# Sums of weight blocks moved beside their own unit's low parts, a cast in two pieces, parts of the first normed columns out of the engines' sequence

## The chip, the cores and the metric

One core of one Trainium2 chip runs the whole program. The metric is the device time of one execution in microseconds, as the median of several runs. One further execution was profiled; the rows below come from it. PE is TensorE (PEld its weight loads), DVE is VectorE, ACT is ScalarE, POOL is GpSimd, SP is SyncE, whose queue issues nearly all transfers.

## What is computed

The reference is one layer of an encoder block on 256 rows of 2048 columns in float32: a half-step feed-forward part, a mixer (causal pooling and gated linear attention), cross attention to 256 memory rows, a second half-step feed-forward part, and a last norm.

```python
x = x + 0.5 * swiglu(rms_norm(x, ffn1_norm[l]), ffn1_w_gate[l], ffn1_w_up[l], ffn1_w_down[l])
h = rms_norm(x, mix_norm[l])
proj = h @ w_in[l]
...
x = x + jnp.concatenate([y_pool, y_gla], axis=-1) @ w_out[l]
x = x + mem_cross_attention(rms_norm(x, xattn_norm[l]), rms_norm(mem, mem_norm[l]),
                            xattn_w_q[l], xattn_w_kv[l], xattn_w_o[l])
x = x + 0.5 * swiglu(rms_norm(x, ffn2_norm[l]), ffn2_w_gate[l], ffn2_w_up[l], ffn2_w_down[l])
...
def swiglu(h, w_gate, w_up, w_down):
    return (jax.nn.silu(h @ w_gate) * (h @ w_up)) @ w_down
```

The feed-forward width is 5632. All weights are float32; 417.58 MB are read from memory in all.

## The kernel before

**Units.** The weights come in as units of 1 MB: a raw tile of 128 partitions by 2048 float32 columns, fetched by SP's queue (L570) into one of three raw buffers. A matmul works on two parts of a number: a high part in the format fp32r and a low part, the remainder. Of a *plain* unit, ACT casts the high part `wh` (L253), DVE subtracts it from the raw weights to make the low part `wl` (L254), and PE does 24 matmuls of 512 columns (L336): high by high, high by low, low by high. `wh` and `wl` have three buffers each, and the split runs two units ahead of the matmuls (`AHEAD`).

**Seven-product units.** In a block of eight units (1024 output columns over 2048 rows of weights), the units of the pairs 0, 2, 4 and 6 are computed by seven block products in place of eight, as in Strassen's scheme: 21 matmuls (L462) in place of 24. For this the weights' four 512-column blocks have to be summed. DVE makes the sums `T` in three additions (L431, one of 1024 and two of 512 columns). The unit's raw blocks 1 to 3 are split as `xh` (ACT) and `xl` (DVE), and `T` as `wh` (ACT) and `wl` (DVE); these last two use the same buffers as a plain unit's. The products P1, P2 and P3 need `xh` and `xl`; P4 to P7 need the parts of `T`. There are 98 such units. The block's order is 0, 1, 2, 3, 4, 6, 5, 7, so seven-product and plain units mostly alternate. At the block's end `combine` (L518 to L523) puts the partial products together and `join` (L533) adds or subtracts them from what the plain units gathered.

**What sets the order.** `Stream` holds the units and the operations between them, in the order of the program. `emit` goes through them and calls, two units ahead of the matmuls, `prepare`, which makes the sums `T` of the *following* unit, and then `split` of the unit itself. So, where a plain unit is followed by a seven-product one, `T` of the latter comes first on DVE, then `wl` of the plain unit; only between two seven-product units is it the other way round. After the split the load of the unit three later is issued; its raw buffer comes free once the split's last reader is done. `in_turn` ties each of these instructions on ACT and DVE behind the one before it. `behind_weights` ties another operation behind the last of them on both engines, and `among_weights` makes it a link of that sequence, so that the splits that come later also stand behind it. What isn't tied is placed by a scheduler.

**Where norms are folded in.** `fold` (L718 to L735) transposes 512 columns of x into a PSUM bank `px` (8 small matmuls, L724) and scales them into high and low parts `xs` (four pairs of L222 on ACT and L223 on DVE). It is called for four chunks of columns, c = 0 to 3, two of them (eight pairs) after the residual of each 1024-column block, and runs beside the next block's units. Its parts are `among_weights`. `Sums.make` builds the sums of activations that the seven products need (`x_sums.make`, called for each of four pairs after a number of units). `gain_columns` clears a tile on DVE (L615) and has a queue fetch gains into it. A first block of the first feed-forward part calls `amid` at one of its quarters.

Of the kernel before, what the change touches and what calls it, by code (L numbers as in the profile page):

```python
# [8 lines left out]
F32R = mybir.dt.float32r  # L9
# [5 lines left out]
P = 128  # L15
# [18 lines left out]
class Stream:  # L34
# [23 lines left out]

    def unit(self, load, f, split=None, prepare=None):
        self.items.append((len(self.units), f))  # L60
        self.units.append((load, split, prepare))
        self.pending = [(n - 1, h) for n, h in self.pending]
        self._flush()

    def emit(self, load, prepare, split):
        done, w, late = -1, {}, []
        for u, f in self.items:
            if u is None:
                f()
                continue  # L70
            ahead = min(u, 1) if u < self.FIRST else self.AHEAD
            while done < min(u + ahead, len(self.units) - 1):
                done += 1
                while late:
                    late.pop(0)()
                after = self.units[done + 1][2] if done + 1 < len(self.units) else None
                both = after and self.units[done][2]
                if not both:
                    prepare(done + 1, after)
                w[done], rest = split(done, self.units[done][1])  # L80
                if both:
                    prepare(done + 1, after)

                def finish(done=done, rest=rest):
                    if rest:
                        rest()
                    if done + self.RAW < len(self.units):
                        load(done + self.RAW)

                if rest:  # L90
                    late.append(finish)
                else:
                    finish()
            f(*w.pop(u))


def build(ctx, tc, I, out):
# [240 lines left out]
    def block_t(srcs, act, evict, delays=(0, 0), amid=None):  # L338
# [6 lines left out]
        def unit(gi):  # L345
            def fn(wh, wl):
                if gi == 0:
                    held["ps"] = [ptile(uid("pt")) for _ in range(2)]
                wh, wl = (w.rearrange("p (k j n) -> p k j n", j=2, n=NB) for w in (wh, wl))
                quarters = [(j, kk) for j in range(2) for kk in range(2)]  # L350
                if amid is not None and gi == 0:
                    quarters.sort(key=lambda q: q[1])
                for n, (j, kk) in enumerate(quarters):
                    if amid is not None and n == (1 if gi else 2):
                        amid(gi)
                    k = 2 * gi + kk
                    for h in range(2):
                        products(held["ps"][j][:, h, :], act, k, h, wh[:, kk, j], wl[:, kk, j],
                                 k == 0, k == n_k - 1)
# [18 lines left out]
    class Sums:  # L378
# [6 lines left out]
        def make(self, g):  # L385
# [18 lines left out]
            )  # L404
            nc.vector.tensor_tensor(out=p12, in0=p12, in1=p22, op=ALU.add)
            done = split(self.tile[:, i, 0], self.tile[:, i, 1], a[:, 4 - n :])
            if self.over:
                done = split(act[:, 2 * g, 0, P:], act[:, 2 * g, 1, P:], p11)
            return done

# [10 lines left out]

    def add_weights(u, raw):
        t = seven_tile("T", 4 * NB, F32, u, 1)
        w = raw.rearrange("p (b n) -> p b n", n=NB)
        v = t.rearrange("p (b n) -> p b n", n=NB)
        for o, a, b in (
            (v[:, 0:2], w[:, 1:3], w[:, 0:1].to_broadcast([P, 2, NB])),
# [3 lines left out]
            in_turn("vector", lambda: nc.vector.tensor_tensor(out=o, in0=a, in1=b, op=ALU.add))  # L431
        return t

    def split_seven(u, raw, t):
        th, tl = (
            wpool.tile([P, 4 * NB], F32R, tag=n, name=f"{n}{u}", bufs=st.AHEAD + 1)
            for n in ("wh", "wl")
        )
        r = [seven_tile(n, 3 * NB, F32R, u, 2) for n in ("xh", "xl")]
        split_weights(*r, raw[:, NB:])  # L440
        split_weights(th, tl, t)
        parts = [x.rearrange("p (b n) -> p b n", n=NB) for x in (th, tl, *r)]

        return [parts], None

# [20 lines left out]
    def block_s(srcs, act, sums, order, evict, merge=None, sevens=None):  # L466
# [71 lines left out]
        for g in order:  # L538
            if g in sevens:
                st.unit(srcs[g], unit_s(g), split_seven, add_weights)  # L540
                if g == sevens[-1]:
# [70 lines left out]
    def gain_columns(names, queue):  # L612
        t = rows["gain"] = scope["pool"].tile([P, P], F32, tag="gain", name=uid("gain"), bufs=2)
        if len(names) > 1:
            behind_weights(lambda: nc.vector.memset(t, 0.0))  # L615
        for name, at, n in names:
# [101 lines left out]
    def fold(c, gain):  # L718
# [12 lines left out]

        among_weights(parts)
        for h in range(2):
# [36 lines left out]
    def ffn(wg, wu, wd, down, amid=None):  # L770
# [37 lines left out]
        for i, g in enumerate(PAIRS):  # L808
            st.op(lambda g=g: among_weights(lambda: x_sums.make(g)), (5, 7, 9, 10)[i])
        for lo, n in FF_PARTS:  # L810
# [610 lines left out]

    raws, summed = {}, {}

    def prepare(u, f):
        if f:
            summed[u] = f(u, raws[u])

# [4 lines left out]
    def split_unit(u, own):  # L1432
        raw = raws.pop(u)
        if own is split_seven:
            return split_seven(u, raw, summed.pop(u))
        parts = [
# [18 lines left out]
    for u in range(st.RAW):  # L1455
        load(u)
    st.emit(load, prepare, split_unit)

# [31 lines left out]
```

## Time and profile before

| what | value |
| --- | --- |
| median of 3 runs | 2138.07 us (2137.77 to 2140.59) |
| profiled execution | 2141.02 us |
| its span, first to last instruction | 2138.9 us |
| mean granted TensorE clock | 0.996 of full speed |
| transfers | 435.95 MB, 204 GB/s on the mean |
| DVE waiting for ACT before `wl` of raw weights | 251.1 us |
| ACT waiting for DVE before the cast of `T` | 186.9 us |

The profile gives, for each engine, the time in which it executes. PE's matmuls are pipelined: one of 512 columns is listed with about 0.39 us, while the next starts 0.23 us after it, so PE's pace is read from starts, not from lengths. "Idle before" an instruction is the time its engine did nothing, with the instruction that ended the wait. An engine that isn't the one waited for may be idle at no cost. In the rows, `wl<-raw,wh` means that `wl` is written from `raw` and `wh`; L253 and the like are lines of the kernel.

### The profile page before, as it was taken

Reading aid. Unit: us, or ns where it says so; the run is one execution under the profiler, and the core shown is the slowest. Engines: PE = TensorE matmul, PEld = TensorE weight load, DVE = VectorE, ACT = ScalarE, POOL = GpSimd, SP = SyncE. Lnnn points to the kernel's source line nnn. Section 1 sums busy time; section 2 is a strip of 40 time slices with the busy share of each in tenths; the row PEclk is TensorE's granted clock in tenths of the full one; section 3 lists DMA queues with packets and bytes.
Section 4 is the critical chain, followed back from the end, with each engine's and each line's share of the span. In section 5 each row is a group of like instructions: output and inputs, shape, how many; then the busy total and the mean of one; then the engine's idle time right before and its main releaser. Section 6 shows DMA issues by size and latency. Waiting matters only on the chain.

```text
span 2138.9 us, 24386 instructions
## 1 busy us (share of the span) xinstructions
PE 2099.3 (98%) x9916; PEld 1746.6 (82%) x9916; DVE 1707.2 (80%) x1538; ACT 1092.8 (51%) x986; POOL 14.1 (1%) x40
## 2 busy tenths in 40 slices
PE   9999999999999999999999999999999999999998
PEld 7778887788888888887888888788778887888886
DVE  6999899988997576677666555769998899989974
ACT  7554455544544545364645434546454555445544
POOL 0000000000000000000000000000000000000001
PEclk9999999999999999999999999999999999999999
DMA  7556665566656565457654555565567655776573
GB/s 256 178 182 231 236 216 196 178 235 236 213 200 237 199 197 183 156 193 243 236 190 160 170 165 172 182 233 178 197 216 236 215 198 172 238 239 216 197 256 118
DMA packets 143608, 435.95 MB, mean 204 GB/s; under 512 B 9860, under 2 KB 13544, under 8 KB 143112
## 3 DMA queue, kind: packets, MB, share of 16 engines
q1 hardware_dynamic: 143464, 434.38, 60.0%
q8 instruction: 78, 1.28, 0.2%
q14 instruction: 34, 0.28, 0.0%
q10 hardware_dynamic: 32, 0.01, 0.0%
HBM read 417.58 MB, written 16.78 MB: 203 GB/s over the span
## 4 chain that ended last, share of the span: by engine, by line
PE 69%; DVE 19%; DMA 6%; issue 3%; ACT 3%; SPq 0%; DVEq 0%; ACTq 0%
PE pt L336 32%; PE pa L321 15%; PE pt L462 9%; DVE wl L254 7%; PE pb L336 6%; DVE T L431 5%; PE pe L336 3%; DMA raw<-in_ffn_w_gate 3%; DMA raw<-in_ffn_w_up 2%; DVE xl L254 2%; ACT wh L253 2%; DVE sg L533 1%; DVE sg L520 1%; DVE sg L793 1%; PE pl L1221 1%
## 5 line engine op out<-in xcount | busy, mean ns | idle before, releaser
L254 DVE TENSOR_TENSOR wl<-raw,wh 128x2048 fp32r<-128x2048 f32 (+2 forms) x284 | 637.9, 2250 | 251.7 <-ACT wh L253 251.1
L253 ACT CAST wh<-raw 128x2048 fp32r<-128x2048 f32 (+2 forms) x284 | 532.4, 1881 | 411.1 <-PE pt L336 216.6
L336 PE MATMUL pt<-wh,xs 128*128 128x512 f32 x1536 | 496.7, 392 | 0.0
L336 PE MATMUL pt<-wh,ys 128*128 128x512 f32 x1440 | 451.5, 391 | 0.0
L336 PEld LDWEIGHTS pt<-wh,xs 128*128 128x128 f32 x1536 | 288.8, 188 | 59.5 <-ACT wh L253 0.2
L336 PEld LDWEIGHTS pt<-wh,ys 128*128 128x128 f32 x1440 | 271.4, 189 | 56.2
L321 PE MATMUL pa<-xs,wh 128*128 128x512 f32 x896 | 315.9, 397 | 0.0
L253 ACT CAST wh<-T 128x2048 fp32r<-128x2048 f32 x98 | 187.5, 1913 | 227.3 <-DVE T L431 186.9
L336 PE MATMUL pt<-wl,xs 128*128 128x512 f32 x768 | 300.8, 392 | 1.1 <-DVE wl L254 1.1
L336 PE MATMUL pt<-wl,ys 128*128 128x512 f32 x720 | 282.0, 392 | 0.0
L321 PE MATMUL pa<-xs,wl 128*128 128x256 f32 x896 | 248.5, 281 | 0.0
L254 DVE TENSOR_TENSOR wl<-T,wh 128x2048 fp32r<-128x2048 f32 x98 | 224.0, 2286 | 13.5 <-ACT wh L253 13.2
L321 PEld LDWEIGHTS pa<-xs,wh 128*128 128x128 f32 x896 | 167.6, 188 | 38.1 <-issue 0.3
L253 ACT CAST xh<-raw 128x1536 fp32r<-128x1536 f32 x98 | 145.1, 1480 | 97.9 <-DMA raw<-in_ffn_w_gate 52.7
L254 DVE TENSOR_TENSOR xl<-raw,xh 128x1536 fp32r<-128x1536 f32 x98 | 171.5, 1750 | 5.0 <-ACT xh L253 5.0
L336 PEld LDWEIGHTS pt<-wl,xs 128*128 128x128 f32 x768 | 144.8, 189 | 31.7 <-DVE wl L254 2.0
L321 PEld LDWEIGHTS pa<-xs,wl 128*128 128x128 f32 x896 | 169.1, 189 | 1.7 <-issue 0.2
L336 PEld LDWEIGHTS pt<-wl,ys 128*128 128x128 f32 x720 | 136.1, 189 | 28.3
L431 DVE TENSOR_TENSOR T<-raw 128x1024 f32<-128x1024 f32 x98 | 119.7, 1221 | 33.7 <-DMA raw<-in_ffn_w_gate 17.3
L462 PE MATMUL pt<-wh,xs 128*128 128x512 f32 x320 | 126.4, 395 | 16.2 <-ACT wh L253 14.9
L431 DVE TENSOR_TENSOR T<-T,raw 128x512 f32<-128x512 f32 x196 | 135.2, 690 | 5.3
L462 PE MATMUL pt<-wh,xe 128*128 128x512 f32 x320 | 123.2, 389 | 0.0
(236 smaller groups left out, 2346.4 us busy)
## 6 DMA issues: line engine op xcount, KB each, us to landing
raw<-in_ffn_w_down SPq DMA_DIRECT2D x88, 1024.0 KB, 5.6
raw<-in_ffn_w_up SPq DMA_DIRECT2D x80, 1024.0 KB, 5.1
raw<-in_ffn_w_gate SPq DMA_DIRECT2D x77, 1024.0 KB, 5.1
raw<-in_w_in SPq DMA_DIRECT2D x32, 1024.0 KB, 5.3
raw<-in_xattn_w_kv SPq DMA_DIRECT2D x32, 1024.0 KB, 5.2
raw<-in_w_out SPq DMA_DIRECT2D x16, 1024.0 KB, 5.6
raw<-in_xattn_w_q SPq DMA_DIRECT2D x16, 1024.0 KB, 5.6
raw<-in_xattn_w_o SPq DMA_DIRECT2D x16, 1024.0 KB, 5.7
```

The lines of the kernel that those rows point to most:

```text
L253: in_turn("scalar", lambda: nc.scalar.copy(hi, src))
L254: in_turn("vector", lambda: nc.vector.tensor_tensor(out=lo, in0=src, in1=f32(hi), op=ALU.subtract))
L321: nc.tensor.matmul(o, w, x, start=k == 0 and i == 0, stop=last and i == 1)
L336: nc.tensor.matmul(ps, a, w, start=first and i == 0, stop=last and i == 2)
L431: in_turn("vector", lambda: nc.vector.tensor_tensor(out=o, in0=a, in1=b, op=ALU.add))
L462: nc.tensor.matmul(banks[n], x, w, start=n in fresh and j == 0, stop=n in ends and j == 2)
L520: nc.vector.tensor_tensor(out=e[:, 1:3], in0=b, in1=e[:, 3:4].to_broadcast([P, 2, NB]), op=ALU.add)
L533: nc.vector.tensor_tensor(out=e, in0=held["ps"][j], in1=e, op=ALU.add if j else ALU.subtract)
L793: nc.vector.scalar_tensor_tensor(out=g[:, h, :], in0=c[:, h, :], scalar=Rcol[:, h : h + 1], in1=g[:, h, :], op0=ALU.mult, op1=ALU.mult,)
L1221: nc.tensor.matmul(ps[:, t, :M], ys[:, 4 * h + d, a, tok], xa["K"][:, d, b, :], start=i == 0, stop=i == 11,)
```

## The change

Four edits. First, `T` is made in `split_seven`, in the unit's own turn, ahead of its `xl` and `wl`; `prepare` and its argument go. Second, the cast of `T` to `wh` is done in two pieces of 1024 columns, of which the first needs only the first of the three additions; `wl` is still one subtraction. Third, the parts of `fold` for c = 0 and 1, the first 1024 columns, are no longer `among_weights`: the scheduler may place them freely. Fourth, smaller things: the first `x_sums.make` comes after four units in place of five and no longer ties the cast on ACT into the sequence, `amid` comes one quarter later in the first unit, and the gain tile is cleared on POOL, tied to nothing. The matmuls are the same in number and kind.

```diff
--- before.py
+++ after.py
@@ -56,13 +56,13 @@
         self.pending.append((after, f))
         self._flush()
 
-    def unit(self, load, f, split=None, prepare=None):
+    def unit(self, load, f, split=None):
         self.items.append((len(self.units), f))
-        self.units.append((load, split, prepare))
+        self.units.append((load, split))
         self.pending = [(n - 1, h) for n, h in self.pending]
         self._flush()
 
-    def emit(self, load, prepare, split):
+    def emit(self, load, split):
         done, w, late = -1, {}, []
         for u, f in self.items:
             if u is None:
@@ -73,13 +73,7 @@
                 done += 1
                 while late:
                     late.pop(0)()
-                after = self.units[done + 1][2] if done + 1 < len(self.units) else None
-                both = after and self.units[done][2]
-                if not both:
-                    prepare(done + 1, after)
                 w[done], rest = split(done, self.units[done][1])
-                if both:
-                    prepare(done + 1, after)
 
                 def finish(done=done, rest=rest):
                     if rest:
@@ -351,7 +345,7 @@
                 if amid is not None and gi == 0:
                     quarters.sort(key=lambda q: q[1])
                 for n, (j, kk) in enumerate(quarters):
-                    if amid is not None and n == (1 if gi else 2):
+                    if amid is not None and n == (1 if gi else 3):
                         amid(gi)
                     k = 2 * gi + kk
                     for h in range(2):
@@ -402,11 +396,11 @@
             nc.vector.scalar_tensor_tensor(
                 out=p22, in0=p11, scalar=-1.0, in1=p22, op0=ALU.mult, op1=ALU.subtract
             )
-            nc.vector.tensor_tensor(out=p12, in0=p12, in1=p22, op=ALU.add)
-            done = split(self.tile[:, i, 0], self.tile[:, i, 1], a[:, 4 - n :])
+            added = nc.vector.tensor_tensor(out=p12, in0=p12, in1=p22, op=ALU.add)
+            split(self.tile[:, i, 0], self.tile[:, i, 1], a[:, 4 - n :])
             if self.over:
-                done = split(act[:, 2 * g, 0, P:], act[:, 2 * g, 1, P:], p11)
-            return done
+                split(act[:, 2 * g, 0, P:], act[:, 2 * g, 1, P:], p11)
+            return None, added
 
         def parts(self, g):
 
@@ -419,29 +413,29 @@
         tag, size, bufs = scope["shared"].get(tag, (tag, n, bufs))
         return scope["pool"].tile([P, size], dt, tag=tag, name=name, bufs=bufs)[:, :n]
 
-    def add_weights(u, raw):
+    def split_seven(u, raw):
+
         t = seven_tile("T", 4 * NB, F32, u, 1)
         w = raw.rearrange("p (b n) -> p b n", n=NB)
         v = t.rearrange("p (b n) -> p b n", n=NB)
+        th, tl = (
+            wpool.tile([P, 4 * NB], F32R, tag=n, name=f"{n}{u}", bufs=st.AHEAD + 1)
+            for n in ("wh", "wl")
+        )
+        rh, rl = (seven_tile(n, 3 * NB, F32R, u, 2) for n in ("xh", "xl"))
         for o, a, b in (
             (v[:, 0:2], w[:, 1:3], w[:, 0:1].to_broadcast([P, 2, NB])),
             (v[:, 2], v[:, 0], w[:, 2]),
             (v[:, 3], v[:, 2], w[:, 3]),
         ):
             in_turn("vector", lambda: nc.vector.tensor_tensor(out=o, in0=a, in1=b, op=ALU.add))
-        return t
-
-    def split_seven(u, raw, t):
-        th, tl = (
-            wpool.tile([P, 4 * NB], F32R, tag=n, name=f"{n}{u}", bufs=st.AHEAD + 1)
-            for n in ("wh", "wl")
-        )
-        r = [seven_tile(n, 3 * NB, F32R, u, 2) for n in ("xh", "xl")]
-        split_weights(*r, raw[:, NB:])
-        split_weights(th, tl, t)
-        parts = [x.rearrange("p (b n) -> p b n", n=NB) for x in (th, tl, *r)]
-
-        return [parts], None
+        split_weights(rh, rl, raw[:, NB:])
+        for c in (slice(0, 2 * NB), slice(2 * NB, 4 * NB)):
+            in_turn("scalar", lambda: nc.scalar.copy(th[:, c], t[:, c]))
+        in_turn("vector", lambda: nc.vector.tensor_tensor(
+            out=tl, in0=t, in1=f32(th), op=ALU.subtract
+        ))
+        return [[x.rearrange("p (b n) -> p b n", n=NB) for x in (th, tl, rh, rl)]], None
 
     def seven(banks, act, sums, g, fresh, ends, weights):
         th, tl, rh, rl = weights
@@ -537,7 +531,7 @@
 
         for g in order:
             if g in sevens:
-                st.unit(srcs[g], unit_s(g), split_seven, add_weights)
+                st.unit(srcs[g], unit_s(g), split_seven)
                 if g == sevens[-1]:
                     st.op(combine if merge else lambda: among_weights(combine))
             else:
@@ -612,7 +606,7 @@
     def gain_columns(names, queue):
         t = rows["gain"] = scope["pool"].tile([P, P], F32, tag="gain", name=uid("gain"), bufs=2)
         if len(names) > 1:
-            behind_weights(lambda: nc.vector.memset(t, 0.0))
+            nc.gpsimd.memset(t, 0.0)
         for name, at, n in names:
             queue.dma_start(t[at : at + n, :], I[name].rearrange("o (k p) -> (o k) p", p=P))
 
@@ -729,7 +723,7 @@
                 done = split_scaled(xs, 4 * c + j, v[:, j, :], gcol(gain + 4 * c + j))
             return done
 
-        among_weights(parts)
+        among_weights(parts) if c >= 2 else parts()
         for h in range(2):
             q = tmp.tile([P, NB], F32, tag="j", name=uid("j"))
             nc.scalar.activation(q, x[:, h], AF.Square, accum_out=ss[:, h, c : c + 1])
@@ -806,7 +800,7 @@
             split(ys[:, k : k + 4, 0, :], ys[:, k : k + 4, 1, :], v)
 
         for i, g in enumerate(PAIRS):
-            st.op(lambda g=g: among_weights(lambda: x_sums.make(g)), (5, 7, 9, 10)[i])
+            st.op(lambda g=g: among_weights(lambda: x_sums.make(g)), (4, 7, 9, 10)[i])
         for lo, n in FF_PARTS:
             whole = n == KT // 4
             for b in range(0, n - 1, 2):
@@ -1419,11 +1413,7 @@
     st.op(close_scope)
 
 
-    raws, summed = {}, {}
-
-    def prepare(u, f):
-        if f:
-            summed[u] = f(u, raws[u])
+    raws = {}
 
     def load(u):
         raws[u] = wpool.tile([P, 4 * NB], F32, tag="raw", name=f"raw{u}", bufs=st.RAW)
@@ -1432,7 +1422,7 @@
     def split_unit(u, own):
         raw = raws.pop(u)
         if own is split_seven:
-            return split_seven(u, raw, summed.pop(u))
+            return split_seven(u, raw)
         parts = [
             wpool.tile([P, 4 * NB], F32R, tag=t, name=f"{t}{u}", bufs=st.AHEAD + 1)
             for t in (("wh",) if own else ("wh", "wl"))
@@ -1454,7 +1444,7 @@
     gain_columns([("ffn1_norm", G_FFN1, 16)], nc.scalar)
     for u in range(st.RAW):
         load(u)
-    st.emit(load, prepare, split_unit)
+    st.emit(load, split_unit)
 
 
 # ---- launch: one core; inputs and outputs as the reference has them ----
```

The order of instructions follows. In its rows the number after a tile's name is the unit (`wl17` is the low part of unit 17), the number after the underscore only tells tiles apart; lines of the changed kernel are 6 lower where functions became shorter.

DVE in the second block of the first feed-forward part, from the joins of one block to the first units of the next. Before:

```order
L254 TENSOR_TENSOR xl16_804<-raw16_703,xh16_803 128x1536
L254 TENSOR_TENSOR wl16_802<-T16_756,wh16_801 128x2048
L533 TENSOR_TENSOR sg44_796<-pt39_583,sg44_796 128x1024
L533 TENSOR_TENSOR sg44_796<-pt40_584,sg44_796 128x1024
L431 TENSOR_TENSOR T18_835<-raw18_764 128x1024
L431 TENSOR_TENSOR T18_835<-T18_835,raw18_764 128x512 x2
L254 TENSOR_TENSOR wl17_840<-raw17_733,wh17_839 128x2048
L254 TENSOR_TENSOR xl18_874<-raw18_764,xh18_873 128x1536
L254 TENSOR_TENSOR wl18_872<-T18_835,wh18_871 128x2048
```

And now:

```order
L431 TENSOR_TENSOR T16_801<-raw16_707 128x1024
L431 TENSOR_TENSOR T16_801<-T16_801,raw16_707 128x512 x2
L248 TENSOR_TENSOR xl16_805<-raw16_707,xh16_804 128x1536
L527 TENSOR_TENSOR sg44_796<-pt39_585,sg44_796 128x1024
L435 TENSOR_TENSOR wl16_803<-T16_801,wh16_802 128x2048
L527 TENSOR_TENSOR sg44_796<-pt40_586,sg44_796 128x1024
L248 TENSOR_TENSOR wl17_841<-raw17_737,wh17_840 128x2048
L431 TENSOR_TENSOR T18_872<-raw18_764 128x1024
L431 TENSOR_TENSOR T18_872<-T18_872,raw18_764 128x512 x2
L248 TENSOR_TENSOR xl18_876<-raw18_764,xh18_875 128x1536
L435 TENSOR_TENSOR wl18_874<-T18_872,wh18_873 128x2048
```

`T18` stood ahead of `wl17`, and `T16` further up, ahead of `wl15`; now each stands directly ahead of `xl` of its own unit, and `wl17` comes right behind the second join (L527, L533 before).

PE at the same place, from the end of unit 16 into unit 17. Before:

```order
L462 MATMUL pt48_884<-xh16_803,xe26_413 128x512
L462 MATMUL pt48_884<-xl16_804,xe26_413 128x512
L462 MATMUL pt48_884<-xh16_803,xe26_413 128x512
L336 MATMUL pt48_884<-wh17_839,xs_107 128x512
L462 MATMUL pt46_882<-wh18_871,xs_107 128x512
L336 MATMUL pt47_883<-wl17_840,xs_107 128x512
L336 MATMUL pt47_883<-wh17_839,xs_107 128x512 x2
L336 MATMUL pt47_883<-wl17_840,xs_107 128x512
```

And now:

```order
L456 MATMUL pt48_890<-xh16_804,xe23_364 128x512
L456 MATMUL pt48_890<-xl16_805,xe23_364 128x512
L456 MATMUL pt48_890<-xh16_804,xe23_364 128x512
L330 MATMUL pt48_890<-wh17_840,xs_107 128x512
L330 MATMUL pt47_889<-wl17_841,xs_107 128x512
L330 MATMUL pt47_889<-wh17_840,xs_107 128x512 x2
L330 MATMUL pt47_889<-wl17_841,xs_107 128x512
```

A product of unit 18 with its summed weights (`wh18`, L462) stood ahead of the first product with `wl17`; it now comes behind the plain unit's products:

```order
L330 MATMUL pt48_890<-wl17_841,xs_107 128x512
L330 MATMUL pt48_890<-wh17_840,xs_107 128x512
L456 MATMUL pt47_889<-xh18_875,xs_107 128x512
L456 MATMUL pt48_890<-xh18_875,xe23_364 128x512
L456 MATMUL pt46_888<-wh18_873,xs_107 128x512
L456 MATMUL pt45_887<-xl18_876,xs_107 128x512
L456 MATMUL pt45_887<-xh18_875,xs_107 128x512
```

ACT in the output projection of the mixer, where the first normed columns for the cross attention are folded in (units 176 to 179). Before:

```order
L735 ACTIVATE j260_7018,ss_100<-x249_6733 128x512
L735 ACTIVATE j261_7020,ss_100<-x249_6733 128x512
L222 ACTIVATE xs_107<-px256_6980,gains_97 128x256 x4
L222 ACTIVATE xs_107<-px259_7001,gains_97 128x256 x4
L253 CAST wh177_7026<-raw177_6880 128x2048
L253 CAST xh178_7061<-raw178_6914 128x1536
L253 CAST wh178_7059<-T178_7022 128x2048
L253 CAST wh179_7092<-raw179_6952 128x2048
```

And now:

```order
L729 ACTIVATE j260_7066,ss_100<-x249_6775 128x512
L434 CAST wh176_6988<-T176_6987 128x1024
L729 ACTIVATE j261_7068,ss_100<-x249_6775 128x512
L247 CAST wh177_7070<-raw177_6927 128x2048
L216 ACTIVATE xs_107<-px256_7028,gains_97 128x256
L216 ACTIVATE xs_107<-px259_7049,gains_97 128x256
```

The cast of the plain unit 177 stood behind all eight evictions of `px` and now stands ahead of them; `xh178` follows the eighth. The cast of `T176` shows as one row for each of its two pieces. On PE the 24 products of unit 177 moved ahead of the products of unit 176 that go into the two banks the evictions empty (`pt263` and `pt264`). Before:

```order
L462 MATMUL pt254_6954<-wh176_6944,ys_108 128x512
L462 MATMUL pt254_6954<-wl176_6945,ys_108 128x512
L462 MATMUL pt254_6954<-wh176_6944,ys_108 128x512
L462 MATMUL pt263_7069<-xh176_6946,ys_108 128x512
L462 MATMUL pt263_7069<-xl176_6947,ys_108 128x512
L462 MATMUL pt263_7069<-xh176_6946,ys_108 128x512
```

And now:

```order
L456 MATMUL pt254_7002<-wh176_6988,ys_108 128x512
L456 MATMUL pt254_7002<-wl176_6989,ys_108 128x512
L456 MATMUL pt254_7002<-wh176_6988,ys_108 128x512
L330 MATMUL pt254_7002<-wh177_7070,ys_108 128x512
L330 MATMUL pt255_7003<-wh177_7070,ys_108 128x512
L330 MATMUL pt254_7002<-wl177_7071,ys_108 128x512
```

## The prediction

> **What bounds the kernel now.** I read the page's first part, then which waits TensorE (PE) has, then the span cut into stretches, and last the single rows at the worst places.
>
> ```profile
> PE 2099.3 (98%) x9916; PEld 1746.6 (82%) x9916; DVE 1707.2 (80%) x1538; ACT 1092.8 (51%) x986; POOL 14.1 (1%) x40
> 219.33 27.20 PE pt L336 x120
> ```
>
> PE is 98% busy. Its pace is set by 512-column matmuls: 27.20 us / 120 = 0.2267 us each (a row of the chain, cut to 200 to 300 us). The change neither adds nor removes a matmul, so it can win only the time in which PE is off this pace. The waits of PE are few (who waits <- for what: us in total, times, longest):
>
> ```profile
> PE pt L462 <- ACT wh L253: 17.6, 14, 2.2
> PE pt L462 <- DVE xs L223: 2.0, 2, 1.8
> PE pt L462 <- DVE xl L254: 1.9, 5, 0.7
> PE pt L462 <- DVE sg L533: 1.8, 3, 0.6
> PE pt L462 <- DVE ys L260: 1.3, 4, 0.3
> PE pt L336 <- DVE wl L254: 1.1, 1, 1.1
> PE pt L462 <- ACT xh L253: 0.9, 2, 0.5
> PE pe L336 <- DVE ys L260: 0.8, 1, 0.8
> ```
>
> These are 32 waits and 27.4 us. Nearly all are at L462, the products of a seven-product unit, and most end with the cast of its summed weights on ScalarE (ACT). By stretches (length, then busy us of PE, PEld, DVE, ACT, POOL, the granted clock, DMA share):
>
> ```profile
> 50.00:200.00 150.00, 142.43 (x625) 115.07 (x624) 140.17 (x123) 79.91 (x60) 0.00 (x0) 0.99 0.58 198
> 200.00:350.00 150.00, 150.00 (x667) 124.25 (x666) 133.43 (x107) 78.21 (x54) 0.00 (x0) 1.00 0.63 220
> 350.00:450.00 100.00, 95.93 (x425) 77.68 (x424) 93.49 (x72) 50.81 (x35) 0.00 (x0) 1.00 0.58 198
> 450.00:700.00 250.00, 249.38 (x1119) 206.07 (x1118) 215.73 (x167) 125.09 (x90) 0.00 (x0) 1.00 0.64 226
> 950.00:1050.00 100.00, 96.14 (x459) 79.70 (x458) 76.58 (x74) 54.00 (x70) 0.00 (x0) 0.98 0.70 243
> 1350.00:1400.00 50.00, 48.15 (x211) 38.97 (x211) 38.78 (x33) 24.87 (x28) 0.00 (x0) 0.97 0.63 213
> 1500.00:1600.00 100.00, 94.76 (x419) 76.60 (x418) 92.67 (x71) 49.13 (x33) 0.00 (x0) 1.00 0.59 199
> 1750.00:1850.00 100.00, 96.68 (x428) 78.42 (x427) 93.56 (x72) 51.02 (x36) 0.00 (x0) 1.00 0.59 200
> 2000.00:2100.00 100.00, 98.86 (x445) 80.87 (x445) 78.63 (x56) 47.98 (x31) 0.00 (x0) 1.00 0.68 232
> ```
>
> Length less PE busy is 7.57, 0, 4.07, 0.62, 3.86, 1.85, 5.24, 3.32, 1.14 us, together 27.7. Four stretches have VectorE (DVE) at 93% or more: gate and up blocks of both feed-forward parts. The two near 1000 and 1390 have it at 77%, so something else stops PE there.
>
> One wait costs more than its idle time. At the worst place (PE, then DVE; start, length, idle before in brackets):
>
> ```profile
> 105.78 0.39 PE L336 MATMUL pt<-wh,xs 128*128 128x512 f32 x1
> 108.41 0.50 PE L462 MATMUL pt<-wh,xs 128*128 128x512 f32 x1 [2.25 <-ACT wh L253]
> 108.75 0.40 PE L336 MATMUL pt<-wl,xs 128*128 128x512 f32 x1
> ```
>
> ```profile
> 101.42 2.34 DVE L533 TENSOR_TENSOR sg<-pt,sg 128x1024 f32<-128x1024 f32 x2
> 103.69 1.21 DVE L431 TENSOR_TENSOR T<-raw 128x1024 f32<-128x1024 f32 x1
> 104.93 1.42 DVE L431 TENSOR_TENSOR T<-T,raw 128x512 f32<-128x512 f32 x2
> 106.27 2.28 DVE L254 TENSOR_TENSOR wl<-raw,wh 128x2048 fp32r<-128x2048 f32 x1
> 108.47 1.75 DVE L254 TENSOR_TENSOR xl<-raw,xh 128x1536 fp32r<-128x1536 f32 x1
> ```
>
> From start to start 2.63 us pass, the next start comes 0.34 later, the pace would be 0.2267 for each: 2.63 + 0.34 - 0.45 = 2.52 lost for 2.25 idle, so 0.27 more a wait, 32 x 0.27 = 8.6 us. Behind such places the granted clock goes down for a moment:
>
> ```profile
> 108.00:112.00 4.00, 3.59 (x10) 2.88 (x11) 4.00 (x3) 2.17 (x2) 0.00 (x0) 0.68 0.57 167
> 112.00:116.00 4.00, 4.00 (x17) 3.26 (x16) 2.56 (x4) 1.49 (x1) 0.00 (x0) 0.89 0.88 346
> 1000.00:1004.00 4.00, 4.00 (x12) 3.16 (x11) 4.00 (x3) 1.06 (x1) 0.00 (x0) 0.57 0.85 222
> ```
>
> The first dip costs 4 x 0.32 + 4 x 0.11 = 1.7 us, the second 4 x 0.43 = 1.7; the stretch of 1350 to 1400 (clock 0.97) has 50 x 0.03 = 1.5, a third. Together 5. All that the change can reach is 27.7 + 8.6 + 5 = **41 us**.
>
> **The change part by part.** *Sums at their own unit.* Before, DVE makes T of the coming seven-product unit ahead of the low part wl of the plain unit that PE needs first. In the rows above, 1.21 + 1.42 us of T (103.69 to 106.27) stand ahead of wl, which ends at 108.55; PE wanted it at 106.0. After, wl follows the joins directly: it runs 103.7 to 105.95 and is just in time. T follows at 105.95, its first add ends at 107.2, the first half of its cast at about 108.3. PE needs that only after the plain unit's other 22 products, 22 x 0.2267 = 5.0, at 111. So 2.5 us go here, and the dip behind them. DVE's work is the same, only its order changes. What is late next: T, xl and wl of one unit come in one piece, 2.63 + 1.75 + 2.28 = 6.7 us, against 24 + 21 products, 45 x 0.2267 = 10.2 us, of PE for a pair of units, with 2.2 more for the plain unit's wl: covered, but at block ends the joins, multiplications and turned casts come on top.
>
> The old order also has DVE wait for transfers, since T needs its raw weights a unit early:
>
> ```profile
> L431 DVE TENSOR_TENSOR T<-raw 128x1024 f32<-128x1024 f32 x98 | 119.7, 1221 | 33.7 <-DMA raw<-in_ffn_w_gate 17.3 <-DMA raw<-in_ffn_w_up 15.0 <-DMA raw<-in_ffn_w_down 0.6
> raw<-in_ffn_w_gate SPq DMA_DIRECT2D x77, 1024.0 KB, 5.1
> SPq L570 <- DVE gain L615: 4.9, 1, 4.9
> ```
>
> A raw buffer comes free with wl of the unit three before, and 5.1 us later the next weights are in. Between that wl and T stood only xl and a wl, 1.75 + 2.28 = 4.0 us: DVE waits 1 us or more. After, one more piece stands between (2.28 of the plain wl, or 2.63 of T): 6.3 us or more, over 5.1. Most of the 33.7 us of DVE idle goes; at 93% busy that is what lets DVE catch up. SyncE's queue no longer stands 4.9 us behind the gain memset, once.
>
> DVE sets a floor by stretch: 140.17 of 150 leaves 9.8 us, 93.49, 92.67 and 93.56 of 100 leave 6.5, 7.3 and 6.4. I take for 50 to 200: loss 7.57 + 6 waits x 0.27 + 1.7 = 10.9, gain 6, since the waits where up parts are multiplied, turned and cast come from DVE's own load. For 350 to 450: 5.4 lost, 5 won; 1500 to 1600: 6.9 and 5; 1750 to 1850: 4.7 and 4.5; the ends (450 to 700, 2000 to 2100): 2.8 and 2.3. Together 22.8.
>
> *Cast in two pieces.* No 128x1024 cast of this kind is in the trace. From
>
> ```profile
> L253 ACT CAST xh<-raw 128x1536 fp32r<-128x1536 f32 x98 | 145.1, 1480 | 97.9 <-DMA raw<-in_ffn_w_gate 52.7
> L253 ACT CAST wh<-T 128x2048 fp32r<-128x2048 f32 x98 | 187.5, 1913 | 227.3 <-DVE T L431 186.9
> ```
>
> 512 columns more cost 0.43, so 1024 cost 1.05 and two pieces 2.10: 98 x 0.19 = 18 us more of ACT, which is 51% busy and idles 227 us ahead of this very cast. Bounds: half of 1.91 each (nothing more) and 1.48 each (1.05 more a unit, 103 us). Estimate 0.19, hidden; uncovered it would show only where PE waits for the second half. The first half is ready 0.86 sooner, at 14 waits up to 12 us; this is inside the 41 and not added again. The cast now waits for T of its own unit; behind it on ACT stands the next plain unit's cast, which PE wants 5 us later.
>
> *Parts of the first normed columns.* At 985 to 1000 (three rows of PE, two of ACT):
>
> ```profile
> 994.88 0.47 PE L462 MATMUL pt<-wh,ys 128*128 128x512 f32 x1 [1.84 <-DVE xs L223]
> 997.43 0.50 PE L462 MATMUL pt<-xh,ys 128*128 128x512 f32 x1 [0.46 <-ACT xh L253]
> 999.31 0.50 PE L462 MATMUL pt<-wh,ys 128*128 128x512 f32 x1 [1.37 <-ACT wh L253]
> 987.19 0.47 ACT L222 ACTIVATE xs<-px,gains 128x256 fp32r<-128x256 f32 x1 [2.77 <-PE px L724]
> 994.12 1.90 ACT L253 CAST wh<-raw 128x2048 fp32r<-128x2048 f32 x1
> ```
>
> PE waits for a PSUM bank that eight evictions empty, and the next unit's cast stands behind them until 994.12, though ACT idled 2.77 us before the first. After, cast and wl go ahead into that idle time, and 24 products of the plain unit, 5.4 us, stand where PE waited 1.84 and less; the evictions ended just before 994.88 and end up to 2.6 us later with T's adds among them, still covered. Loss 3.86 + 4 x 0.27 + 1.7 = 6.6, gain 6; at 1386 the same with 1.85 + 2 x 0.27 + 1.5 = 3.9, gain 3.9. If the evictions came more than 3.5 us later (5.4 - 1.84), the excess would be the price.
>
> *The rest.* Sums of activations one unit earlier, a later call in the first unit, the memset on GpSimd: no row of PE waits for them; between -1 and +1 us, taken as nothing, hidden by the 50-us first stretch's DVE slack.
>
> Sum: 22.8 + 6 + 3.9 = 32.7, less about 1 for new short waits: **-32 us**. The profiled execution has 2141.0 (2.1 outside the span) and would have 2109; the median of the runs is 2138.1, so **2106**, 1.5% less.
>
> The Trainium skill's page "TensorE: Matmul & The Clock Gate", section "HAM oscillation — how this bites in real kernels", has the clock fall after idle gaps over some 3.4 us. Here it falls to 0.68 in the 4 us behind a gap of 2.25, so the trace disagrees. By that rule the dips would not hang on these gaps (the third rival below).
>
> **The rivals.**
> 1. DVE stays the bound: the waits move from wl of the plain unit to xl and wl of the seven-product unit, as 93% busy suggests; against it, 200 to 350 has 89% and no loss. Half of 22.8 goes: 32 - 11.4 = 20.6, **2118**.
> 2. Everything comes back, the DVE floors allowing it but for 1 us: **2097**.
> 3. The dips in the clock stay though the gaps go: 32 - 5 = 27, **2111**.
> 4. Slower: T, its first add and first half of the cast are 1.22 + 1.05 = 2.27 us; if DVE comes to T only when PE starts the unit, the unit's nine products without T (2.04) cover all but 0.23, and each of 98 units waits 0.23 + 0.27: 49 us, less the 10 of the two folds, +39, **2177**. It decides once DVE has no lead of a unit; the idle DVE time of 33.7 speaks against it.
> 5. The change does not do what it says: waits only change their names, within 4 us of 2138.
>
> **How the numbers follow.** Forecast 0.50 (by itself 2101 to 2113), rivals 0.20, 0.12, 0.10, 0.04, 0.04. The range reaches from all 41 won (2097, less 1) to half of the forecast (16 us, 2122). 0.2% is 4.3 us, about what a measurement can tell from nothing: faster 0.92, same 0.04, slower 0.04.
>
> **What would show it.** T should no longer wait for transfers (33.7 to a few us); PE's 14 waits for the cast should fall to 5 or fewer; PE should be fully busy from 985 to 1000 and 1380 to 1390, with clock 1.00 there; DVE's busy time should stay. Wrong if PE's waits reappear at L462 for xl or wl, if ACT's casts of T pass 2.5 us a unit, or if weight transfers land later than 5.1 us because they start closer together.

## The result, and the profile after

The changed kernel takes 2121.42 us (median of 4 runs, 2120.72 to 2124.74) against 2139.33 of the kernel before in the same series: ratio 0.9919, 95% interval 0.9902 to 0.9937. That is 17.9 us less, where 32 were forecast. A second series, e12 below, gave 2121.87 against 2142.08, ratio 0.9908 (0.9895 to 0.9922).

Of the waits of PE in the changed kernel's profile (L456 are the products of a seven-product unit, L527 the joins at a block's end), these stand in place of the 32 of before:

```profile
PE pt L456 <- DVE sg L527: 10.0, 4, 2.5
PE pt L456 <- DVE xl L248: 4.5, 9, 1.4
PE pe L330 <- DVE ys L254: 1.4, 1, 1.4
```

No wait for the cast of T is left, nor one for wl. But the joins, 1.8 us in three waits before, now have 10.0 in four. The groups of instructions on DVE and ACT (last column: idle ahead of them, and what ended it):

```profile
L431 DVE TENSOR_TENSOR T<-raw 128x1024 f32<-128x1024 f32 x98 | 119.4, 1218 | 0.5
L435 DVE TENSOR_TENSOR wl<-T,wh 128x2048 fp32r<-128x2048 f32 x98 | 223.8, 2284 | 2.1 <-ACT wh L434 1.8
L434 ACT CAST wh<-T 128x1024 fp32r<-128x1024 f32 x196 | 205.7, 1053 | 331.2 <-DVE T L431 301.2
```

T waits for transfers no longer: 33.7 us of idle became 0.5, as forecast. Each half of the cast takes 1.053 us, as estimated. The stretches of the span, with the columns as before:

```profile
50.00:200.00 150.00, 145.32 (x645) 118.68 (x644) 141.62 (x128) 82.22 (x72) 0.00 (x0) 0.99 0.59 201
350.00:450.00 100.00, 97.16 (x427) 79.38 (x426) 92.42 (x70) 52.14 (x42) 0.00 (x0) 0.98 0.58 194
450.00:700.00 250.00, 249.68 (x1129) 206.88 (x1128) 214.12 (x167) 129.62 (x109) 0.32 (x1) 1.00 0.65 226
950.00:1050.00 100.00, 99.64 (x499) 83.80 (x498) 77.21 (x78) 61.88 (x95) 0.00 (x0) 1.00 0.74 255
1350.00:1400.00 50.00, 49.63 (x226) 40.56 (x225) 38.30 (x33) 26.76 (x30) 0.00 (x0) 1.00 0.64 215
1500.00:1600.00 100.00, 97.14 (x436) 79.61 (x435) 92.40 (x78) 52.08 (x43) 0.00 (x0) 0.98 0.62 203
1750.00:1850.00 100.00, 97.17 (x436) 79.66 (x435) 92.47 (x78) 54.47 (x45) 0.00 (x0) 0.98 0.63 209
2000.00:2100.00 100.00, 98.26 (x444) 80.67 (x443) 70.35 (x48) 44.62 (x32) 0.00 (x0) 1.00 0.63 210
```

Around 1000 and 1390 PE is busy to 0.4 us, and the clock is 1.00: the gain forecast for these two places came in (which edit brings it, e1, e6 and e8 show). In four stretches of the feed-forward parts 2.8 to 4.7 us of idle are left, and in three of them the granted clock is 0.98 where it was 1.00. One of the four places where PE waits for a join, first PE, then DVE:

```profile
399.57 0.40 PE L456 MATMUL pt<-xh,xs 128*128 128x512 f32 x1
402.49 0.50 PE L456 MATMUL pt<-wh,xs 128*128 128x512 f32 x1 [2.52 <-DVE sg L527]
```

```profile
396.75 1.22 DVE L527 TENSOR_TENSOR sg<-pt,sg 128x1024 f32<-128x1024 f32 x1
397.89 2.28 DVE L248 TENSOR_TENSOR wl<-raw,wh 128x2048 fp32r<-128x2048 f32 x1
400.08 1.21 DVE L431 TENSOR_TENSOR T<-raw 128x1024 f32<-128x1024 f32 x1
401.22 1.21 DVE L527 TENSOR_TENSOR sg<-pt,sg 128x1024 f32<-128x1024 f32 x1
```

The second join frees the PSUM bank that PE's next product needs. It stands behind the low part of a plain unit, which PE reaches only at 407, and behind the first addition of T. The same happens near 1532 and 1790; near 140 it is the first join that PE waits for, and it stands behind the low part alone. Each time it is the end of the second gate block of a part (of the three parts of a feed-forward layer two have two such blocks), where DVE also makes low parts of the turned columns of the blocks before (`ys`). And behind each of the four the clock went down in this execution:

```profile
400.00:404.00 4.00, 1.51 (x5) 1.24 (x6) 4.00 (x5) 2.66 (x4) 0.00 (x0) 0.89 0.65 210
404.00:408.00 4.00, 4.00 (x14) 3.15 (x13) 3.97 (x5) 1.64 (x2) 0.00 (x0) 0.68 0.13 52
```

With the prediction's own measures: idle over its stretches is 16.0 us (27.7 before), 14 waits x 0.27 are 3.8, four dips x 1.7 are 6.8, together 26.6, where the forecast left 41 - 32 = 9. The four joins alone are 10.0 + 4 x 0.27 + 6.8 = 17.9, about the whole difference of 17.6 (that as many us were won is chance). The profiled execution (2124.74 us, clock 0.995) is 3 to 4 us longer than the three others (2120.72 to 2121.72, clock 0.997).

### The profile page after: what moved, and what is told of

Same layout as the page of the kernel before. It is cut to its first block, busy times and chain, and to the rows that moved or that the text cites. A ratio compares the mean times of both kernels' runs of the same rounds, so it can differ in the third digit from the quotient of the medians.

```text
span 2122.9 us, 24500 instructions
## 1 busy us (share of the span) xinstructions
PE 2095.6 (99%) x9916; PEld 1748.2 (82%) x9916; DVE 1705.0 (80%) x1537; ACT 1108.7 (52%) x1084; POOL 14.3 (1%) x41
## 4 chain that ended last, share of the span: by engine, by line
PE 82%; DVE 13%; issue 2%; ACT 1%; DMA 1%; SPq 0%; DVEq 0%; ACTq 0%
PE pt L330 39%; PE pt L456 15%; PE pa L315 15%; PE pb L330 6%; DVE wl L248 3%; PE pe L330 3%; DVE T L431 3%; DVE wl L435 2%; DVE xl L248 2%; DVE sg L527 1%; DVE sg L787 1%; PE pl L1215 1%; PE pv L1250 1%; PE ph L797 0%; PE px L718 0%
## 5 line engine op out<-in xcount | busy, mean ns | idle before, releaser
L434 ACT CAST wh<-T 128x1024 fp32r<-128x1024 f32 x196 | 205.7, 1053 | 331.2 <-DVE T L431 301.2
L247 ACT CAST xh<-raw 128x1536 fp32r<-128x1536 f32 x98 | 144.9, 1479 | 27.7 <-PE pt L456 22.6
L456 PE MATMUL pt<-wh,xs 128*128 128x512 f32 x320 | 126.8, 396 | 7.6 <-DVE sg L527 7.6
L456 PE MATMUL pt<-wh,xe 128*128 128x512 f32 x320 | 124.6, 395 | 0.0
L456 PE MATMUL pt<-xh,xs 128*128 128x512 f32 x320 | 120.4, 396 | 2.5 <-DVE sg L527 2.5
```

The source lines that it names most:

```text
L247: in_turn("scalar", lambda: nc.scalar.copy(hi, src))
L434: in_turn("scalar", lambda: nc.scalar.copy(th[:, c], t[:, c]))
L456: nc.tensor.matmul(banks[n], x, w, start=n in fresh and j == 0, stop=n in ends and j == 2)
```

## The experiments

Each kernel's time is given beside the runs of before in its own series (2141.81 us for e1 to e4, 2140.86 for e5 to e8, 2142.08 for e9 to e12), and as the ratio to them.

**e1, the folds alone** (on the kernel before):

```diff
-        among_weights(parts)
+        among_weights(parts) if c >= 2 else parts()
```

> The kernel before with one edit: the parts of the first 1024 normed columns out of the sequence. Theory A (the two folds near 990 and 1385 gave what the prediction took for them, 6 and 3.9 us): 9 to 10 us less than before, about 2129. Rival (the gain there needs the new place of T too, since the next unit's T and casts stand behind the evictions): 4 us less or nothing, 2135 or more.

2132.83 us, 9.0 less, ratio 0.9961 (0.9949 to 0.9974). Theory A holds: the two folds are worth this much without T's new place.

**e2, T at its own unit alone** (the changed kernel with the other edits taken back):

```diff
-        for c in (slice(0, 2 * NB), slice(2 * NB, 4 * NB)):
-            in_turn("scalar", lambda: nc.scalar.copy(th[:, c], t[:, c]))
-        in_turn("vector", lambda: nc.vector.tensor_tensor(
-            out=tl, in0=t, in1=f32(th), op=ALU.subtract
-        ))
+        split_weights(th, tl, t)
```

> The change without its other parts: T at its own unit, its cast in one piece, folds and the small edits as before. Theory A (17.9 us won in all, of which 10 by the folds): 8 us less than before, about 2131, with four waits of PE for the second kind of addition at block ends (join) of about 2.5 us each. Rival (the order of T needs the cast in two pieces, or else the first product with T waits 0.86 us longer in its unit): nothing won or slower, 2139 or more.

2147.61 us, 5.8 *more* than before, ratio 1.0028 (1.0016 to 1.0039). Theory A fell. The group on DVE and the longest entry of PE's waits say why:

```profile
L248 DVE TENSOR_TENSOR wl<-T,wh 128x2048 fp32r<-128x2048 f32 x98 | 224.6, 2291 | 33.7 <-ACT wh L247 33.7
```

```profile
PE pt L452 <- DVE xl L248: 16.1, 9, 2.2
```

The old order had DVE wait 33.7 us for transfers ahead of T; the new one has it wait 33.7 us for the cast ahead of wl. T, the cast and wl now follow each other within a unit, and only xl (1.75 us) lies beside a cast of 1.91. PE sees the lost time at nine places, at eight of which two seven-product units follow each other and xl of the second is late.

**e3, one cast** (the changed kernel with the edit of e2's diff alone):

> The changed kernel with the cast of T in one piece again, 98 casts fewer. Theory A (after the change no wait of PE ends with this cast, so its halves are worth little): within 4 us of the changed kernel, 2118 to 2126, ACT busy 16 to 19 us less. Rival (the halves carry the gain, 14 waits of 0.86 us): 12 us slower than the changed kernel, about 2133.

2139.22 us, 15 to 18 over the changed kernel (by the ratios to before, and by the times), ratio to before 0.999 (0.9981 to 0.9999). Theory A fell again; the rival had the sign, but not the place:

```profile
L248 DVE TENSOR_TENSOR wl<-T,wh 128x2048 fp32r<-128x2048 f32 x98 | 224.6, 2292 | 34.8 <-ACT wh L247 34.7
```

```profile
PE pt L452 <- DVE xl L248: 14.7, 9, 2.2
PE pt L452 <- DVE sg L523: 10.1, 6, 2.6
```

The halves pay on DVE, 34.8 us of waits against 2.1, and PE sees it as late xl (14.7 us against 4.5).

**e5, the two pieces alone** (the kernel before with the cast in two pieces, e2's diff the other way):

> The kernel before with the cast of T in two pieces as its only edit. Theory B, formed on the two runs with one cast (in them DVE waits 33.7 and 34.8 us for the cast ahead of wl of the sums, with two pieces 2.1: in the new order T, xl and wl of one unit follow each other, and xl with 1.75 us does not hide a cast of 1.91 and its signal; so the pieces pay only where the cast lies on DVE's path): little, 0 to 5 us less than before, DVE's wait for the cast falls from 13.5 us. Rival (the pieces pay at PE, whatever the order: 14 waits of 0.86 us): about 12 us less than before.

2140.38 us, ratio 0.9998 (0.9989 to 1.0007): nothing. PE's 14 waits for the cast became, among its waits,

```profile
PE pt L336 <- DVE wl L254: 15.4, 14, 2.0
```

so they only changed their name: behind the cast PE needed wl of the plain unit, which T still held up. The rival's 14 x 0.86 us weren't there to win.

**e6, order and pieces** (the changed kernel without the folds and the small edits):

> The change without the folds and the small edits: T at its own unit and its cast in two pieces. Theory B: the run with the order alone stood 6 us over before for DVE's 33.7 us of waits for the cast; the pieces take these away, so 8 to 10 us less than before (the whole change less the 8 of the folds), DVE's wait ahead of wl of the sums at 2 to 3 us. Rival (the folds or the small edits made up for the order): at or above before.

2129.70 us, 11.2 less, ratio 0.9945 (0.9931 to 0.9958). The order alone costs 6, the pieces alone give nothing, both together give 11. One stretch in its windows:

```profile
950.00:1050.00 100.00, 99.16 (x487) 82.82 (x486) 77.82 (x76) 58.79 (x85) 0.00 (x0) 1.00 0.74 254
```

PE's idle near 1000 is mostly gone (3.86 us before, 0.84 here) though the folds are as before. So the gains of order and folds overlap, and do not add up: one by one they are 11.2 and 9.0, both together 13.6 (e8).

**e7, xl ahead of T**:

```diff
+        split_weights(rh, rl, raw[:, NB:])
         for o, a, b in (
...
-        split_weights(rh, rl, raw[:, NB:])
```

> The changed kernel with xh and xl ahead of the three additions of T in a unit, all else the same. Theory B (xl is what hides the second piece of the cast on DVE): DVE waits some 0.9 to 1.2 us ahead of wl of the sums in each of 98 units, 90 us or more in all, and the time rises by 10 us or more over the changed kernel, 2131 or more. Rival (the nine waits of PE for xl, 4.5 us, are there because T stands ahead of xl; DVE has room for the rest): 4 to 7 us less than the changed kernel.

2193.15 us, ratio 1.0245 (1.0231 to 1.0259), 71 over the changed kernel. Theory B holds, the rival is out:

```profile
L435 DVE TENSOR_TENSOR wl<-T,wh 128x2048 fp32r<-128x2048 f32 x98 | 224.5, 2291 | 96.1 <-ACT wh L434 94.3 <-PE pt L330 1.8
```

With nothing beside the second half of the cast, DVE waits 96.1 / 98 = 0.98 us in every unit.

**e8, the small edits undone** (`x_sums.make` after five units and tied to ACT's sequence, the gain tile cleared on DVE, `amid` a quarter earlier):

> The changed kernel with the small edits taken back: the first sums of activations after five units and tied to ACT's sequence too, the gain tile cleared on DVE behind the weights, the call in the first block a quarter earlier. Theory (the prediction's: they are worth nothing, between -1 and +1 us): 2119 to 2124. Rival (the gain tile's clearing held SyncE's queue 4.9 us, and the sums stand in DVE's way): 3 us or more above the changed kernel.

2127.24 us, ratio 0.9937 (0.9925 to 0.995), 13.6 less than before and 4 to 6 over the changed kernel. The prediction's "nothing" was wrong. Beside e6, which lacks the folds too, it also shows that these add only 2.5 us once the order is changed.

**e10, the tie alone; e11, the later call alone.** The tie, put back into the changed kernel:

```diff
-            split(self.tile[:, i, 0], self.tile[:, i, 1], a[:, 4 - n :])
+            done = split(self.tile[:, i, 0], self.tile[:, i, 1], a[:, 4 - n :])
...
-            return None, added
+            return done
```

> The changed kernel with one small edit taken back: the sums of activations tie their cast into ACT's sequence again, so that the next plain unit's cast stands behind it. Theory C (of the small edits this one counts: with all taken back, wl of a plain unit came 1.6 us late near 70, its cast standing at 67.96 right behind the sums' at 67.76, where the changed kernel has it at 60.89): 4 to 6 us over the changed kernel, with that wait back. Rival (the earlier call does it): within 2 us of the changed kernel.

> The changed kernel with the first sums of activations after five units in place of four, the tie to ACT's sequence left out as in the change. Theory C (the untying counts, not the earlier call): within 2 us of the changed kernel. Rival: 4 to 6 us over it.

e10 took 2128.72 us (ratio 0.9945, 0.9931 to 0.9958), 6.9 over e12, the changed kernel in this series; e11 took 2124.04 (0.9917, 0.9904 to 0.9931), 2.2 over it, which the intervals can't tell from the 2 expected or from nothing. So the untying counts. In e10, one row each of ACT (two), DVE and PE:

```profile
68.52 0.30 ACT L253 CAST xs<-j 128x128 fp32r<-128x128 f32 x1 [3.75 <-DVE j L394]
68.72 1.90 ACT L247 CAST wh<-raw 128x2048 fp32r<-128x2048 f32 x1
70.66 2.29 DVE L248 TENSOR_TENSOR wl<-raw,wh 128x2048 fp32r<-128x2048 f32 x1 [0.99 <-ACT wh L247]
73.00 0.50 PE L330 MATMUL pt<-wl,xs 128*128 128x512 f32 x1 [1.59 <-DVE wl L248]
```

ACT idles 3.75 us for the sums, the plain unit's cast stands behind them, and the delay goes on to DVE and PE. Untied, that cast runs ahead of the sums, at 60.89 in the changed kernel. This one wait is a part of the 6.9; the rest is spread over other short waits, xl among them (6.3 us in eleven, 4.7 in ten in e12). In the kernel before the same cast stood behind the sums too, from 67.44 to 69.35, but DVE was at T until 71.05: the tie cost nothing until T had moved away.

**e4, the joins first** (added to the changed kernel; `link` is set for the second gate block of a part, and `ahead` is 1 for its last unit):

```diff
+            def add():
+                return None, nc.vector.tensor_tensor(
+                    out=e, in0=held["ps"][j], in1=e, op=ALU.add if j else ALU.subtract
+                )
+            among_weights(add) if link else add()
```

> The changed kernel with one addition: at the end of the second gate block of a part (four places) the joins become links of DVE's sequence, so that they stand ahead of wl of the next plain unit and of T. Theory A (the missing 14 us lie in four waits of PE for the joins, 2.7 us from start to start each, and a dip of the clock of 1.7 behind each): those four waits fall under 0.5 us, the dips go, 10 to 17 us less than the changed kernel, 2104 to 2111. Rival (DVE is simply full there; a join moved ahead makes wl and xl late by as much): the waits change their names, 2118 or more.

2117.09 us, ratio 0.9887 (0.9873 to 0.99), some 4 to 7 less than the changed kernel: less than theory A said, more than the rival allowed. PE's waits:

```profile
PE pt L457 <- ACT wh L435: 5.4, 2, 2.7
PE pt L457 <- DVE xl L249: 4.5, 9, 1.3
...
PE pt L457 <- DVE sg L529: 0.6, 2, 0.3
```

The joins' 10.0 us fell to 0.6. At two of the four places another wait came up, for the first half of the next cast, since T's first addition still stood behind wl of the plain unit.

**e9, the joins and then T** (e4, with T's first addition ahead of that wl at the four places):

```diff
+                if done - 2 in self.late:
+                    start(done + 1)
                 w[done], rest = split(done, self.units[done][1])
```

> The kernel with the joins first (2117.1 us), with one more edit at the same four places: the first addition of T stands directly behind the joins, ahead of wl of the plain unit. Theory C (the changed kernel's order left two things late at these places, the joins and the first half of the cast; with the joins first, PE waited 2.7 us for that cast at two of the four): the two waits fall under 1 us, with a dip of the clock less, 4 to 7 us less than with the joins alone, 2110 to 2113, and no wait of PE over 1.5 us is left but one near 80. Rival (DVE has no room there; what is moved ahead makes something else late by as much): 2116 or more, with waits for wl or xl in their place.

2115.41 us, ratio 0.9877 (0.9864 to 0.9891), 6.5 less than e12 and the fastest of all. PE's longest waits in it:

```profile
PE pt L469 <- DVE xl L251: 4.5, 9, 1.4
PE pt L333 <- DVE wl L251: 1.6, 3, 0.5
...
PE pt L469 <- ACT wh L447: 1.2, 1, 1.2
PE pt L469 <- DVE ys L257: 1.1, 1, 1.1
PE pt L469 <- DVE sg L541: 1.0, 3, 0.4
```

Beside e4 it gained some 2 us, not 4 to 7: of the two waits for the cast, 5.4 us, one of 1.2 is left, and the three of wl at 0.5 are new, so the rival has a part of the truth. Its mean clock is 0.999, without a dip before PE's work ends.

**e12, the changed kernel again**:

> The changed kernel itself, beside the three others: 2120 to 2123 us, so that differences of a few us to it are read on the same chip. The granted clock in its profile should dip for some 3 us behind one or more of the four waits for the joins; if dips follow these gaps by no fixed rule, their number may differ from the four of the first profile.

2121.87 us. The four waits for joins are there again, 10.2 us, but only two dips follow them in its profile (why, the last section shows).

## Why the prediction was wrong in size

**What bounds the kernel.** Right: the same matmuls, the gain made of PE's waits and dips, and DVE's 33.7 us of waits for transfers gone.

**T at its own unit.** Here the term of 22.8 failed. Its step "wl follows the joins directly" was read at one place, the joins of the block near 101, and taken for all blocks. In four others the order on DVE is wl or T's first addition *ahead* of a join. The prediction named joins "on top" at block ends, but priced only leftovers of the old waits there, and no new one. By its own measures, the stretches of this term lost 30.7 us before, and in the changed kernel's profile they lose 15.3 + 12 x 0.27 + 6.8 = 25.3: 5.4 were won in place of 22.8. The four joins are 17.9 of what is lost there. In e9, where joins and T are moved, the same stretches lose 9.3 + 16 x 0.27 = 13.6, so that 17.1 of the 22.8 are won; its profiled execution is 10.4 us shorter than that of the changed kernel, and its median 6.5 below e12, whose profile has two of the four dips. Against the runs of before in its own series e9 wins 26.7 of the 32. Where the last 5.3 lie no run shows; its profile has nine waits for xl, 4.5 + 9 x 0.27 = 6.9 us, where the prediction took about 1 for new short waits.

**The cast.** The time that the pieces add on ACT was hidden, as said (ACT is busy 1108.7 us, 1092.8 before). Their gain was "not added again", as a part of what the order wins; but without them the order wins nothing: it is 6 us slower (e2). The step looked at PE's waits and at ACT's idle time, not at DVE, which after the change waits for the cast in the same unit. The slower rival had this chain, T and cast in the unit's own turn, but made PE wait for T directly; the runs show DVE waiting, and PE for xl.

**The folds.** Right in mechanism and size, taken by themselves (9.9 forecast, 9.0 in e1). Beside the new order they are worth 2.5 (e8 against e6), since the order takes most of the same waits.

**The rest.** "Nothing" was wrong: 4 to 6 us (e8), all of it, within the noise, by the untying of the sums' cast on ACT (e10). That no row of PE waited for the sums was true of the kernel before, where T hid the delay; with the tie kept it is not true of the new order (e10).

**The rivals.** The first, half of the feed-forward gain lost to DVE (2118), came nearest, with the wrong waits: the nine for xl, which the prediction had named as a sign against itself, are 4.5 us, the joins 10. The third, dips that stay without gaps, is out: near 1000 and 1390 the dips went with the gaps, and e9 has none.

## What to carry to other kernels

When work moves from one place of an in-order engine to another, look at every place where that engine also serves something else (here the joins), not at one typical place. A removed wait is only a gain once the chain that takes its place is hidden too: ask what lies beside each step of it on *each* engine, and split a step (the cast) where its neighbour is a little too short to cover it. A tie that costs nothing now may do so only because something slower stands beside it (the sums' cast beside T): price it again in the new order.

## What the runs showed of the hardware

The clock's dips do not follow gaps by their length alone. At the same place near 400 the changed kernel's gap of 2.52 us was followed by 0.89 and 0.68, while e4, with a gap of 2.70 there, has

```profile
396.00:400.00 4.00, 2.39 (x11) 1.63 (x9) 4.00 (x4) 2.57 (x6) 0.00 (x0) 1.00 0.13 26
400.00:404.00 4.00, 2.91 (x13) 2.41 (x14) 3.97 (x5) 1.51 (x2) 0.00 (x0) 1.00 0.74 250
```

What decides is where the gap falls. In each profile the dips while PE has work last 3.41 us, or twice that, and start whole multiples of 3.413 us apart: in the kernel before at 109.44, 1000.31 and 1389.43, which is 261 and 114 steps. So the span can be cut into windows of 3.41 us by a grid that the dips give (the one behind PE's last product included), and that lies elsewhere in each execution. Of e12, the windows at its four waits for joins:

```profile
138.76:142.17 3.41, 2.12 (x10) 1.43 (x8) 3.41 (x2) 3.41 (x4) 0.00 (x0) 1.00 0.92 299
142.17:145.58 3.41, 1.89 (x7) 1.23 (x7) 3.41 (x4) 2.21 (x4) 0.00 (x0) 1.00 0.62 190
398.17:401.58 3.41, 0.89 (x5) 0.42 (x4) 3.41 (x4) 2.27 (x4) 0.00 (x0) 1.00 0.38 85
1531.40:1534.81 3.41, 1.61 (x7) 0.95 (x6) 3.41 (x3) 2.31 (x4) 0.00 (x0) 1.00 0.41 97
1534.81:1538.23 3.42, 2.71 (x12) 2.25 (x13) 3.42 (x4) 2.00 (x3) 0.00 (x0) 1.00 0.73 279
1787.40:1790.81 3.41, 1.11 (x5) 0.56 (x3) 3.41 (x3) 2.30 (x4) 0.00 (x0) 1.00 0.34 60
```

The two gaps that lie in one window (2.52 and 2.30 us idle) have a dip from the end of that window on; the two that the grid cuts (1.29 and 1.52, 1.80 and 0.71) have none. In the changed kernel's first profile all four lay in one window each (2.33 to 2.52 us idle); the gap of 2.70 in e4 is cut into 1.04 and 1.66. Over all 14 profiles, from 20 us on, the 32 windows with 1.95 us or more of idle all have a dip behind them, of the 68 with 1.2 to 1.95 us 17 have, and of those with less none. What decides between 1.2 and 1.95 stays open.

The changed kernel had four dips behind its four waits in one profile and two in the other. So a gap of 2 to 3 us costs a dip of 1.7 us more (half the clock for 3.41 us) or not by where the grid lies, and this part of a stall's price varies from run to run; in these profiles gaps under 1.2 us, one to a window, cost none.
